# Second feed-forward of a two-layer flow step: products ordered around two row statistics

## The chip, the cores and the metric

The kernel runs on one core of a Trainium2 chip. The metric is the device time of one execution in microseconds (us). Five engines work side by side, each from its own queue in order: TensorE for matmuls (PE, with its weight loads as PEld), VectorE (DVE), ScalarE (ACT), GpSimd (POOL), and SyncE (SP), which issues most transfers. PE accumulates into PSUM, and DVE and ACT read the results from there. Everything is float32. A precise product is made of three matmuls: each operand is split into a rounded part ("hi") and a remainder ("lo"), and hi x hi, hi x lo and lo x hi are added up.

## The reference

One step of a hybrid backbone with two layers over 640 tokens (512 latent, 128 prompt) and a width of 1024. The first layer mixes by attention, the second by a gated linear recurrence; each is followed by a SwiGLU feed-forward with 2816 hidden columns. The change lies in the second layer's feed-forward and in the final norm behind it:

```python
def _rms_norm(x, g):
    xf = x.astype(jnp.float32)
    y = xf * lax.rsqrt(jnp.mean(xf * xf, axis=-1, keepdims=True) + RMS_EPS)
    return (y * g.astype(jnp.float32)).astype(x.dtype)

def _modulate(x, g, shift, scale):
    return _rms_norm(x, g) * (1 + scale[:, None, :]) + shift[:, None, :]

def _swiglu(x, w_gu, w_down):
    gate, up = jnp.split(x @ w_gu, 2, axis=-1)
    return (jax.nn.silu(gate) * up) @ w_down
...
        f_l = _swiglu(_modulate(lat, norm_g[i, 1], sh2_l, sc2_l), ffn_w_gu[i], ffn_w_down[i])
        ctx = ctx + g2_c[:, None, :] * f_c
        lat = lat + g2_l[:, None, :] * f_l
    y_prompt = _rms_norm(ctx, final_g)
    y_sample = _rms_norm(lat, final_g)
```

## The kernel before

Activations lie transposed: the 1024 features as 8 tiles of 128 partitions, the tokens along the free axis. The stages run one after another: attention, first feed-forward, recurrence, second feed-forward. Weights arrive as 512 KB blocks in the buffers `raw` (three of them), and ACT makes the rounded part, DVE the remainder.

**Who sets the order.** The program is written as one sequence. A planner then gives each engine its queue: among the instructions that its own estimate of time holds ready, it takes the one that was written first. The queues are fixed before the run, and semaphores are set between engines where data demands it. `tc.issue_after(ins)` adds an order without data: what is written inside the block stands behind `ins` on the same engine's queue. It adds no wait on another engine.

**The row statistic** (`stat`, line 376). The squares of the 8 feature tiles are made by ACT (`square`, L371) and added by DVE into `ssq` (L373); the last tile's square stays apart as `lastq`. For every 128 tokens, two matmuls with a column of ones sum over the partitions into the PSUM tile `at` (L382 for `ssq`, L385 for `lastq`). DVE makes the variance `var` (L387), POOL takes it to the power -0.5 (L389, `rs`), DVE spreads it on a diagonal `dg` (L391), and matmuls with ones (L394) put the factor on all partitions in a PSUM tile.

**The opening of the second feed-forward** (`project_halves`, then `ffn_halves`). The tokens are halved, 0 to 320 and 320 to 640, and each half has its own statistic. While the output projection of the second half ends, the first half is normalised already (`first_half`). Then the second statistic comes, ACT copies its factor to `rt` (L740), and `second_half` normalises the second half: 16 DVE products (`normed`, L691), 16 ACT shifts (L692), and the splits (`halve`, L1011 on ACT, L1012 on DVE).

The 22 hidden tiles are pairs of a gate tile and an up tile. The first two pairs (`PLAIN`) are multiplied in the usual way by `plain(us, c)` for token half `c`: four products of 24 matmuls per half (L835 to L837). From the third pair on a block scheme with seven instead of eight products is used (L779 to L781, `product`): `pair_a` needs the gate weights and the first token half alone, `pair_b` and `pair_c` need sums of weights, S1 to S4, and sums of activations, T1 to T4. `sums(k)` makes the T of feature tile k: L711 to L713 on DVE, one difference on POOL (L714), and four splits. `sum_weights` loads the up tile, makes the S with four operations (L762) and splits them into the buffers `whx`, `wlx`. For the third pair the S are made on DVE, behind the statistic's `dg` (argument `self.dg`); for all later ones on POOL, behind the operation kept in `self.pw`, which is the statistic's power.

In the written sequence stand: `plain` for the first half, `pair_a` of the third pair, `second_half`, `plain` for the second half, `sum_weights` of the third pair, `sums`; then for each pair `pair_b` and `pair_c`, and after every few pairs a part of the down projection (`project_part`).

**The end** (`project_last`). The last part of the down projection runs over 384 tokens, then over 256. Each group has its residual additions (L425 in `residual`), squares and a statistic. The final products (L466: x times factor times `final_g`, one per feature tile and token group) stand behind `self.added`, the last residual addition written. Each two feature tiles leave with one transfer (L468).

Of the kernel before, what the change touches and what calls it, by code (L numbers as in the profile page):

```python
# [12 lines left out]
ALU = mybir.AluOpType  # L13
AX = mybir.AxisListType

P = 128
D = 1024
# [13 lines left out]
EPS = 1e-6  # L31
# [8 lines left out]
KH = KT // 2  # L40
# [3 lines left out]
PLAIN = 2  # L44
# [77 lines left out]
def _pieces(t0, t1):  # L122
    return [(s, max(a, t0), min(b, t1)) for s, a, b in ((0, 0, NLAT), (1, NLAT, NTOK)) if max(a, t0) < min(b, t1)]


class _Step:
# [249 lines left out]
    def stat(self, t0, t1):  # L376
        nc = self.nc
        bl = [min(b, t1 - P) for b in range(t0, t1, P)]
        n = len(bl)
        ps = self.ps()  # L380
        for j, b in enumerate(bl):
            nc.tensor.matmul(ps[:, j:j + 1], self.ssq[:, b:b + P], self.ones[:, 0:1], start=True, stop=not self.lastq)  # L382
            if not self.lastq:
                continue
            nc.tensor.matmul(ps[:, j:j + 1], self.lastq[t0][:, b - t0:b - t0 + P], self.ones[:, 0:1], start=False, stop=True)  # L385
        v = self.t([P, 8], F32, "var", 2)[:, 0:n]
        nc.vector.tensor_scalar(v, ps[:, 0:n], 1.0 / D, EPS, ALU.mult, ALU.add)  # L387
        r = self.t([P, 8], F32, "rs", 2)[:, 0:n]
        self.pw = nc.gpsimd.tensor_tensor(r, v, self.mhalf.broadcast_to([P, n]), ALU.pow).ins  # L389
        dg = self.t([P, 4, P], F32, "dg", 1, self.sb)[:, 0:n]  # L390
        self.dg = nc.vector.tensor_tensor(dg, self.ident.unsqueeze(1).broadcast_to([P, n, P]), r.unsqueeze(2).broadcast_to([P, n, P]), ALU.mult).ins  # L391
        ps = self.ps("rr" if "rr" in self.ptags else "mx")
        for j, b in enumerate(bl):
            mm = nc.tensor.matmul(ps[:, b - t0:b - t0 + P], self.ones, dg[:, j], start=True, stop=True)  # L394
        self.r = ps, t0
        return mm.ins
# [25 lines left out]
    def residual(self, f, t0, t1, ps, G, sq):  # L422
        for s, a, b in _pieces(t0, t1):
            xs = self.x[:, f, a:b]
            self.added = self.nc.vector.scalar_tensor_tensor(xs, ps[:, a - t0:b - t0], G[:, s, f:f + 1], xs, ALU.mult, ALU.add).ins  # L425
        if sq:
            self.square(f, t0, t1)

# [21 lines left out]
    def project_last(self, w, hi, lo, gk):  # L450
        G = self.need(self.gcols, gk)
        us, fin = [], []
        for f in range(0, KT, 2):
            us += self.two(w[f:f + 2], f % 4)
        for c, (t0, t1) in enumerate(CHL):
            for f, u in enumerate(us):
                with self.tc.issue_after(mm) if c and f == KT - 1 else nullcontext():
                    ps = self.chunk(u, hi, lo, t0, t1)
                self.residual(f, t0, t1, ps, G, True)
            mm = self.stat(t0, t1)  # L460
            fin.append((t0, t1, self.r[0]))
        for t0, t1, r in fin:
            for k in range(KT):
                xs = self.x[:, k, t0:t1]
                with self.tc.issue_after(self.added):
                    self.nc.vector.scalar_tensor_tensor(xs, xs, self.col("fg", k), r[:, 0:t1 - t0], ALU.mult, ALU.mult)  # L466
                if k % 2:
                    self.nc.sync.dma_start(self.o["y"][k * P - P:k * P + P, t0:t1].rearrange("(k p) t -> p k t", p=P), self.x[:, k - 1:k + 1, t0:t1])  # L468
# [217 lines left out]
    def normed(self, k, t0, t1, key):  # L686
        nc = self.nc
        A, B = [self.need(self.AB, key + (j,)) for j in range(2)]
        for s, a, b in _pieces(t0, t1):
            v = self.x[:, k, a:b]  # L690
            nc.vector.scalar_tensor_tensor(v, v, A[:, s, k:k + 1], self.rt[:, a:b], ALU.mult, ALU.mult)  # L691
            nc.scalar.activation(v, v, AF.Identity, bias=B[:, s, k:k + 1])  # L692

    def halve(self, n, k, v):
# [12 lines left out]
    def sums(self, k, xd):  # L707
        nc = self.nc
        b11, b12, b21, b22 = [self.x[:, j, a:a + HT] for j in (k, k + KH) for a in (0, HT)]
        t2 = self.t([P, HT], F32, "c22", 2, self.sb)  # L710
        nc.vector.tensor_tensor(b11, b12, b11, ALU.subtract)  # L711
        nc.vector.tensor_tensor(t2, b22, b11, ALU.subtract)
        nc.vector.tensor_tensor(b12, b22, b12, ALU.subtract)  # L713
        nc.gpsimd.tensor_tensor(b21, b21, t2, ALU.subtract)  # L714
        for n, v in (("T1", b11), ("T2", t2), ("T3", b12), ("T4", b21)):
            self.halve(n, k, v)
        for j in (k, k + KH):
            nc.sync.dma_start(self.x[:, j], xd[j * P:j * P + P])
# [50 lines left out]
    def last_weights(self, q):  # L769
        hi, lo = [self.t([P, KH, P], F32R, n, 1, self.sb) for n in ("wuh", "wul")]  # L770
        self.split(hi, lo, q["u"][:, KH:])
        q["W"]["A22"] = hi, lo

    def product(self, ps, W, X, start):
        nc = self.nc
        hi, lo = W
        xh, xl = self.X[X + "h"], self.X[X + "l"]
        for k in range(KH):
            nc.tensor.matmul(ps, hi[:, k], xh[:, k], start=start and k == 0, stop=False, skip_group_check=not start)  # L779
            nc.tensor.matmul(ps, hi[:, k], xl[:, k], start=False, stop=False, skip_group_check=not start)  # L780
            nc.tensor.matmul(ps, lo[:, k], xh[:, k], start=False, stop=(k == KH - 1), skip_group_check=not start)  # L781

# [43 lines left out]
        self.hidden(q["j"], 1, q["c22"], self.total(q["c"], q["u2"], "g"))  # L826

    def plain(self, us, c):
        nc = self.nc
        for j, pair in enumerate(us):  # L830
            for u, (hi, lo) in enumerate(pair):
                ps = self.pg()[:, 0:HT]
                for k in range(KT):
                    xh, xl = [self.X[f"B{1 + k // KH}{1 + c}{p}"][:, k % KH] for p in "hl"]
                    nc.tensor.matmul(ps, hi[:, k], xh, start=(k == 0), stop=False)  # L835
                    nc.tensor.matmul(ps, hi[:, k], xl, start=False, stop=False)
                    nc.tensor.matmul(ps, lo[:, k], xh, start=False, stop=(k == KT - 1))  # L837
                if u:
                    self.hidden(j, c, ps, g)
                else:  # L840
                    g = self.t([P, HT], F32, "g", 3, self.sb)
                    nc.scalar.activation(g, ps, AF.Silu)

    def ffn_halves(self, l, key, xd):
        us = [[self.unit(self.i["gu"][l, c * NF + f]) for c in range(2)] for f in range(PLAIN)]
        self.plain(us, 0)
        self.wx, self.share = 0, False
        qs = [None] * PLAIN + [self.gate_weights(l, PLAIN)]
        self.pair_a(qs[PLAIN])
        for k in range(KH):  # L850
            self.second_half(k, key)
        self.plain(us, 1)
        self.sum_weights(qs[PLAIN], self.dg)
        for k in range(KH):
            self.sums(k, xd)
        f0 = 0
        for ci, n in enumerate(CHN):
            for j in range(n):
                f = f0 + j
                if f < PLAIN:  # L860
                    continue
                if f == len(qs):
                    qs.append(self.gate_weights(l, f))
                    self.pair_a(qs[f])
                if j:
                    if f > PLAIN:
                        self.sum_weights(qs[f])
                    if qs[f - 1]:
                        self.pair_c(qs[f - 1])
                    self.last_weights(qs[f])  # L870
                self.pair_b(qs[f], j)
            self.pair_c(qs[f])
            w = self.i["dn"][l, :, :, f0:f0 + n]
            f0 += n
            if f0 == NF:
                self.share = True
                self.project_last(w, self.hhi, self.hlo, (l, 5))
            else:
                qs.append(self.gate_weights(l, f0))
                self.pair_a(qs[f0])  # L880
                self.sum_weights(qs[f0])
                self.last_weights(qs[f0])
                self.project_part(w, self.hhi, self.hlo, (l, 5))
# [280 lines left out]
```

## Time and profile before

| | us |
|---|---|
| median of 3 runs | 1559.88 |
| lowest and highest | 1555.52, 1560.43 |
| profiled execution | 1555.75 |
| its span, first to last instruction | 1554.0 |
| PE busy | 1486.2 (96%) |
| DVE busy | 1076.6 (69%) |
| ACT busy | 716.7 (46%) |
| POOL busy | 208.9 (13%) |

The mean granted TensorE clock over the span is 0.984. In a timeline each row has the start in us from the span's start, the duration in us, the engine, the line, the operation, the tile written and those read, the shapes, and how many like instructions were merged; in brackets stands how long the engine was idle before it, and who released it. A table of stretches gives for each stretch its length, the busy time and number of instructions of each engine asked for (in the order PE, PEld, DVE, ACT, POOL where all are), the granted clock, the busy share of the DMA engines and GB/s. The row of a group of transfers ends with the median time from issue to landing. Consecutive matmuls overlap, so their durations exceed the distance of their starts.

### The profile page before, as it was taken

What the parts mean: (1) busy time and instruction counts of PE and PEld (TensorE: products, weight loads), DVE (VectorE), ACT (ScalarE), POOL (GpSimd) and SP (SyncE); (2) the same over time, 40 slices, a digit from 0 to 9 for tenths busy, and PEclk for the clock granted to TensorE, in tenths of its full rate; (3) what the DMA queues carried; (4) which work ended last, traced back from release to release, by engine and by line L of the source; (5) the groups of instructions that cost most, each with busy time, mean ns of one, the idle gap of its engine ahead of it and who ended that gap; (6) DMA issues with size and microseconds to landing.
All of it is one profiled execution on the core that took longest, in us unless ns stands there. A gap on an engine that the chain in (4) does not pass through costs nothing.

```text
span 1554.0 us, 26047 instructions
## 1 busy us (share of the span) xinstructions
PE 1486.2 (96%) x10303; PEld 1439.7 (93%) x10303; DVE 1076.6 (69%) x2043; ACT 716.7 (46%) x1326; POOL 208.9 (13%) x231
## 2 busy tenths in 40 slices
PE   6999999989999999999999999969999999999996
PEld 4899999879999999999999888869899999999995
DVE  5678788959999987434446489875876665555645
ACT  4576666654332123212334499754544342425241
POOL 2111123100111110000000000000132323232300
PEclk8999999999999999999999999989999999999998
DMA  9545655535666664222223222124242231313111
GB/s 374 161 114 165 178 167 165 155 120 181 193 190 188 208 198 117 74 82 80 64 84 105 70 62 68 55 102 148 69 143 81 70 109 55 109 55 109 55 55 68
DMA packets 69753, 188.25 MB, mean 121 GB/s; under 512 B 7792, under 2 KB 23296, under 8 KB 69504
## 3 DMA queue, kind: packets, MB, share of 16 engines
q1 hardware_dynamic: 57824, 144.49, 29.7%
q0 software_dynamic: 11520, 41.95, 8.8%
q8 instruction: 81, 1.33, 0.4%
q14 instruction: 40, 0.33, 0.1%
q10 hardware_dynamic: 288, 0.16, 0.0%
HBM read 171.09 MB, written 8.92 MB: 116 GB/s over the span
## 4 chain that ended last, share of the span: by engine, by line
PE 79%; DVE 7%; ACT 7%; DMA 3%; issue 3%; POOL 1%; SPq 0%; POOLq 0%; DVEq 0%; ACTq 0%
PE mm L209 13%; PE mm L210 13%; PE mm L211 13%; PE mx L211 5%; PE mx L210 5%; PE mx L209 5%; PE mx L779 3%; PE mx L780 3%; PE mx L781 3%; PE op L629 2%; PE tp L553 1%; PE mc L779 1%; PE mc L781 1%; PE mc L780 1%; PE mm L225 1%
## 5 line engine op out<-in xcount | busy, mean ns | idle before, releaser
L209 PE MATMUL mm<-big,whi 128*128 128x320 f32 (+2 forms) x1290 | 401.2, 314 | 19.0 <-ACT big L1011 10.4
L210 PE MATMUL mm<-big,whi 128*128 128x320 f32 (+2 forms) x1290 | 403.7, 313 | 1.7 <-DVE big L1012 1.2
L211 PE MATMUL mm<-big,wlo 128*128 128x320 f32 (+2 forms) x1290 | 402.4, 313 | 1.0 <-DVE wlo L178 1.0
L209 PEld LDWEIGHTS mm<-big,whi 128*128 128x128 f32 x1290 | 244.2, 190 | 24.2 <-ACT big L1011 11.3
L210 PEld LDWEIGHTS mm<-big,whi 128*128 128x128 f32 x1290 | 245.2, 190 | 4.9 <-DVE big L1012 3.7
L211 PEld LDWEIGHTS mm<-big,wlo 128*128 128x128 f32 x1290 | 244.9, 190 | 2.5 <-DVE wlo L178 1.4
L239 DVE SCALAR_TENSOR_TENSOR mprod<-mraw,csb 128x1024 f32<-128x1024 f32 x160 | 195.8, 1224 | 14.4 <-DMA mraw<-in_wm 13.6
L425 DVE SCALAR_TENSOR_TENSOR x<-mm,G,x 128x128 f32<-128x128 f32 (+3 forms) x211 | 84.9, 435 | 88.2 <-PE mm L211 87.3
L177 ACT CAST whi<-raw 128x1024 fp32r<-128x1024 f32 (+1 forms) x89 | 92.3, 1037 | 111.8 <-PE mm L210 79.0
L178 DVE TENSOR_TENSOR wlo<-raw,whi 128x1024 fp32r<-128x1024 f32 (+1 forms) x89 | 109.1, 1226 | 28.3 <-ACT whi L177 25.8
L211 PE MATMUL mm<-big,wlx 128*128 128x320 f32 (+3 forms) x363 | 112.6, 311 | 0.0
L210 PE MATMUL mm<-big,whx 128*128 128x320 f32 (+3 forms) x363 | 112.6, 310 | 0.0
L209 PE MATMUL mm<-big,whx 128*128 128x320 f32 (+3 forms) x363 | 112.4, 310 | 0.0
L235 POOL DMA_DIRECT2D mraw<-in_wm x80 | 43.3, 542 | 385.1 <-DVE mprod L239 271.0
L389 POOL TENSOR_TENSOR rs<-var,mhalf 128x3 f32<-128x3 f32 (+3 forms) x10 | 9.2, 926 | 584.1 <-DVE var L387 584.1
L209 PE MATMUL mx<-big,whi 128*128 128x320 f32 (+3 forms) x278 | 86.6, 312 | 1.0 <-DVE big L638 1.0
L211 PE MATMUL mx<-big,wlo 128*128 128x320 f32 (+3 forms) x278 | 86.3, 310 | 0.0
L210 PE MATMUL mx<-big,whi 128*128 128x320 f32 (+3 forms) x278 | 86.2, 310 | 0.0
L177 ACT CAST whx<-raw 128x1024 fp32r<-128x1024 f32 (+1 forms) x39 | 40.0, 1028 | 89.3 <-PE mm L210 54.3
L211 PE MATMUL mx<-big,wlx 128*128 128x320 f32 (+3 forms) x245 | 76.1, 310 | 0.4 <-DVE wlx L178 0.4
L210 PE MATMUL mx<-big,whx 128*128 128x320 f32 (+3 forms) x245 | 75.8, 309 | 0.0
L209 PE MATMUL mx<-big,whx 128*128 128x320 f32 (+3 forms) x245 | 75.7, 309 | 0.0
(283 smaller groups left out, 3622.2 us busy)
## 6 DMA issues: line engine op xcount, KB each, us to landing
raw<-in_gu SPq DMA_DIRECT2D x88, 512.0 KB, 3.6
mraw<-in_wm POOLq DMA_DIRECT2D x80, 512.0 KB, 4.0
raw<-in_dn SPq DMA_DIRECT2D x24, 512.0 KB, 3.7
raw<-in_wqk SPq DMA_DIRECT2D x16, 512.0 KB, 5.1
raw<-in_wi SPq DMA_DIRECT2D x16, 512.0 KB, 3.5
raw<-in_dn SPq DMA_DIRECT2D x16, 448.0 KB, 3.3
sw<-in_wm SPq DMA_DIRECT2D x10, 512.0 KB, 10.6
raw<-in_wv SPq DMA_DIRECT2D x8, 512.0 KB, 3.8
```

Source lines behind the costliest of these rows:

```text
L177: nc.scalar.copy(hi, raw)
L178: nc.vector.tensor_tensor(lo, raw, hi.bitcast(F32), ALU.subtract)
L209: nc.tensor.matmul(ps, hi[:, k], xhi[:, k, s], start=(k == 0), stop=False)
L210: nc.tensor.matmul(ps, hi[:, k], xlo[:, k, s], start=False, stop=False)
L211: nc.tensor.matmul(ps, lo[:, k], xhi[:, k, s], start=False, stop=(k == nk - 1))
L235: nc.gpsimd.dma_start(w, self.i["wm"][l * 6 + j - 2, f])
L239: nc.vector.scalar_tensor_tensor(prod, w, 1.0, self.csb[:, s], ALU.mult, ALU.mult, accum_out=out[:, s, f:f + 1])
L425: self.added = self.nc.vector.scalar_tensor_tensor(xs, ps[:, a - t0:b - t0], G[:, s, f:f + 1], xs, ALU.mult, ALU.add).ins
L629: mm = nc.tensor.matmul(out, v, w, start=start, stop=stop)
L779: nc.tensor.matmul(ps, hi[:, k], xh[:, k], start=start and k == 0, stop=False, skip_group_check=not start)
L780: nc.tensor.matmul(ps, hi[:, k], xl[:, k], start=False, stop=False, skip_group_check=not start)
L781: nc.tensor.matmul(ps, lo[:, k], xh[:, k], start=False, stop=(k == KH - 1), skip_group_check=not start)
```

## The change

Three orders are altered; no arithmetic, buffer or transfer is added or removed.

1. The final products (L466) stand behind the variance of the last statistic written (`self.var`) instead of behind the last residual addition.
2. In `plain` for the first token half and in `pair_a` of the third pair, the first matmul of each product stands behind the last L385 matmul of the second half's statistic (`self.at`). Of the very first product only the second half of the contraction does so; its first 12 matmuls stay free.
3. The third pair's S stand on DVE behind the last product of the normalisation (`self.last`) and are written after `sums(0)`. `self.pw` now also takes POOL's difference in `sums`, so that the fourth pair's S stand on POOL behind the last of the four differences.

```diff
-            nc.tensor.matmul(ps[:, j:j + 1], self.lastq[t0][:, b - t0:b - t0 + P], self.ones[:, 0:1], start=False, stop=True)
+            self.at = nc.tensor.matmul(ps[:, j:j + 1], self.lastq[t0][:, b - t0:b - t0 + P], self.ones[:, 0:1], start=False, stop=True).ins
...
-        nc.vector.tensor_scalar(v, ps[:, 0:n], 1.0 / D, EPS, ALU.mult, ALU.add)
+        self.var = nc.vector.tensor_scalar(v, ps[:, 0:n], 1.0 / D, EPS, ALU.mult, ALU.add).ins
...
-            self.added = self.nc.vector.scalar_tensor_tensor(xs, ps[:, a - t0:b - t0], G[:, s, f:f + 1], xs, ALU.mult, ALU.add).ins
+            self.nc.vector.scalar_tensor_tensor(xs, ps[:, a - t0:b - t0], G[:, s, f:f + 1], xs, ALU.mult, ALU.add)
...
-                with self.tc.issue_after(self.added):
+                with self.tc.issue_after(self.var):
                     self.nc.vector.scalar_tensor_tensor(xs, xs, self.col("fg", k), r[:, 0:t1 - t0], ALU.mult, ALU.mult)
...
-            nc.vector.scalar_tensor_tensor(v, v, A[:, s, k:k + 1], self.rt[:, a:b], ALU.mult, ALU.mult)
+            self.last = nc.vector.scalar_tensor_tensor(v, v, A[:, s, k:k + 1], self.rt[:, a:b], ALU.mult, ALU.mult).ins
...
-        nc.gpsimd.tensor_tensor(b21, b21, t2, ALU.subtract)
+        self.pw = nc.gpsimd.tensor_tensor(b21, b21, t2, ALU.subtract).ins
...
+    def held(self, here):
+        return self.tc.issue_after(self.at) if here and self.hold else nullcontext()
+
...
         for k in range(KH):
-            nc.tensor.matmul(ps, hi[:, k], xh[:, k], start=start and k == 0, stop=False, skip_group_check=not start)
+            with self.held(k == 0):
+                nc.tensor.matmul(ps, hi[:, k], xh[:, k], start=start and k == 0, stop=False, skip_group_check=not start)
...
-        nc = self.nc
+        nc, first = self.nc, True
...
-                    nc.tensor.matmul(ps, hi[:, k], xh, start=(k == 0), stop=False)
+                    with self.held(k == (KH if first else 0)):
+                        nc.tensor.matmul(ps, hi[:, k], xh, start=(k == 0), stop=False)
...
+                first = False
...
+        self.hold = True
         self.plain(us, 0)
         self.wx, self.share = 0, False
         qs = [None] * PLAIN + [self.gate_weights(l, PLAIN)]
         self.pair_a(qs[PLAIN])
+        self.hold = False
         for k in range(KH):
             self.second_half(k, key)
         self.plain(us, 1)
-        self.sum_weights(qs[PLAIN], self.dg)
         for k in range(KH):
             self.sums(k, xd)
+            if k == 0:
+                self.sum_weights(qs[PLAIN], self.last)
```

## The prediction

> **What bounds the kernel now.** I read the page first, then the table of stretches around the second feed-forward's opening and around the end, then the timelines of TensorE (PE), VectorE (DVE), ScalarE (ACT) and GpSimd (POOL) in both places.
>
> ```profile
> span 1554.0 us, 26047 instructions
> PE 1486.2 (96%) x10303; PEld 1439.7 (93%) x10303; DVE 1076.6 (69%) x2043; ACT 716.7 (46%) x1326; POOL 208.9 (13%) x231
> ```
>
> PE is busy nearly throughout, so an edit gains only where PE stands or runs slowly. The change touches two such places. The first, in order of time on PE and DVE (start, duration, engine, line):
>
> ```profile
> 1090.04 0.30 PE L835 MATMUL mm<-big,whi 128*128 128x320 f32 x1
> 1098.54 0.28 PE L382 MATMUL at<-ones,ssq 128*128 128x1 f32 x2
> 1099.57 0.36 PE L385 MATMUL at<-ones,sq 128*128 128x1 f32 x2
> 1103.69 0.83 PE L394 MATMUL mx<-dg,ones 128*128 128x128 f32 x6
> 1113.61 0.63 PE L836 MATMUL mm<-big,whi 128*128 128x320 f32 x1 [3.66 <-DVE big L1012]
> ...
> 1093.37 1.08 DVE L373 TENSOR_TENSOR ssq<-ssq,sq 128x320 f32<-128x320 f32 x2
> 1101.63 0.68 DVE L762 TENSOR_TENSOR sum<-raw 128x512 f32<-128x512 f32 x1
> 1104.64 1.22 DVE L1012 TENSOR_TENSOR wlx<-sum,whx 128x1024 fp32r<-128x1024 f32 x1 [0.39 <-ACT whx L1011]
> 1105.78 6.96 DVE L691 SCALAR_TENSOR_TENSOR x<-x,A,r 128x192 f32<-128x192 f32 x16
> 1104.56 0.43 ACT L740 COPY r<-mx 128x320 f32<-128x320 f32 x1
> ```
>
> The squares are summed at 1093.37 + 1.08 = 1094.45, but the statistic's matmuls start at 1098.54: they stand in PE's queue behind products that were ready earlier. The normalisation (L691) starts at 1105.78, and PE runs dry waiting for it. What the dry spell costs is in the stretches (length, PE busy, count, granted clock, DMA):
>
> ```profile
> 1090.00:1098.50 8.50, 8.50 (x60) 1.00 0.24 83
> 1099.90:1103.70 3.80, 3.80 (x28) 1.00 0.00 0
> 1109.95:1113.60 3.65, 0.00 (x0) 0.86 0.00 0
> 1113.60:1118.00 4.40, 4.39 (x16) 0.50 0.00 0
> 1118.00:1119.40 1.40, 1.40 (x7) 0.50 0.00 0
> ```
>
> PE stands for 3.65 us and then runs at clock 0.50 for 5.8 us, in which it does 23 matmuls. At 3.80/28 = 0.136 to 8.50/60 = 0.142 us each these need 3.2 us, so 2.6 us are lost to the clock. The opening loses 3.65 + 2.6 = 6.25 us.
>
> The second place is the end:
>
> ```profile
> 1536.76 4.28 DVE L466 SCALAR_TENSOR_TENSOR x<-x,cols,mx 128x384 f32<-128x384 f32 x8
> 1540.95 0.42 DVE L373 TENSOR_TENSOR ssq<-ssq,sq 128x256 f32<-128x256 f32 x1
> 1541.29 0.60 DVE L425 SCALAR_TENSOR_TENSOR x<-mx,G,x 128x128 f32<-128x128 f32 x2
> 1544.82 0.16 DVE L387 TENSOR_SCALAR var<-at 128x2 f32<-128x2 f32 x1 [1.96 <-PE at L385]
> 1545.80 0.43 DVE L391 TENSOR_TENSOR dg<-ident,rs 128x256 f32<-128x256 f32 x1 [0.82 <-POOL rs L389]
> 1547.60 3.22 DVE L466 SCALAR_TENSOR_TENSOR x<-x,cols,mx 128x256 f32<-128x256 f32 x8 [1.38 <-PE mx L394]
> ...
> 1536.61 0.42 ACT L371 ACTIVATE sq<-x 128x256 f32<-128x256 f32 x1 [0.64 <-DVE ssq L373]
> ...
> 1542.92 0.58 PE L382 MATMUL at<-ones,ssq 128*128 128x1 f32 x2 [5.66 <-DVE ssq L373]
> 1544.22 0.56 PE L385 MATMUL at<-ones,sq 128*128 128x1 f32 x2
> ```
>
> PE's last product ends at 1542.92 - 5.66 = 1537.26. DVE, however, is inside eight final products of the first 384 tokens, 4.28 us, and takes up the last sums only at 1540.95.
>
> **The change part by part.**
>
> *Final products behind the second variance (L466).* The edge puts no semaphore in; it moves eight instructions on DVE's queue from before the last sums to after `var`. The sums then start when their square is there, 1536.61 + 0.42 = 1537.03, not at 1540.95: 3.9 us earlier. The last residuals move from 1541.29 to 1537.4, after PE's end at 1537.26, so that is allowed, and the statistic starts at about 1542.92 - 3.9 = 1539.0. Its four pairs took 1544.78 - 1542.92 = 1.86 us. They ran at the low clock; the first statistic's six pairs show the other price:
>
> ```profile
> 1527.39 0.28 PE L382 MATMUL at<-ones,ssq 128*128 128x1 f32 x2
> 1528.43 0.36 PE L385 MATMUL at<-ones,sq 128*128 128x1 f32 x2
> 1537.20:1542.90 5.70, 0.06 (x1) 0.00 (x0) 5.45 (x13) 0.72 (x2) 0.00 (x0) 0.68 0.72 260
> 1542.90:1546.40 3.50, 1.90 (x9) 1.84 (x9) 0.59 (x2) 0.00 (x0) 0.70 (x1) 0.50 0.07 26
> ```
>
> Six pairs in 1528.79 - 1527.39 = 1.40 us, so four need about 0.9. The wait is now 1.7 us instead of 5.66, and I take the full clock: `var` at 1539.95. What follows it on DVE is 0.16 + 4.28 + 0.43 + 3.22 = 8.1 us without a hole: the holes before `dg` (0.82) and before the second products (1.38) are covered by the 4.28. DVE ends at 1548.05 instead of 1547.60 + 3.22 = 1550.82: 2.8 us gained. At the low clock it is 1.8. So the end does not gain the 4.28: that work comes back after `var` and only fills 2.2 us of holes. The results leave in eight transfers, the larger four of them:
>
> ```profile
> out_y<-x SPq DMA_DIRECT2D x4, 384.0 KB, 2.5
> ```
>
> They now start after 1541 and follow one another at the pace of two products, 2 x 4.28/8 = 1.07 us. At 260 GB/s over a share of 0.72, hence some 360 GB/s when busy, one (0.393 MB) takes 1.09 us; they keep up, and what lies behind the last transfer stays as it is.
>
> *Products behind the statistic (L779, L835).* Again an order alone. Before the statistic there remain the first product's first twelve matmuls, 12 x 0.142 = 1.7 us from 1090.04. PE then waits from 1091.75 to 1094.45 for the squares: 2.7 us, a loss that was not there. Behind it are 108 matmuls (84 of the plain products, 24 of the third pair's), 15.3 us of cover at 0.142 for the chain through `var`, POOL's power, `dg`, L394, the copy and the normalisation.
>
> Does the wait halve the clock? The trace of before has two nearer gaps:
>
> ```profile
> 1018.00:1021.40 3.40, 0.68 (x5) 0.42 (x4) 2.15 (x3) 3.35 (x6) 0.00 (x0) 1.00 0.48 154
> 1021.40:1025.00 3.60, 3.60 (x25) 3.60 (x26) 3.30 (x4) 3.57 (x4) 0.00 (x0) 1.00 0.00 0
> 941.00:945.00 4.00, 0.99 (x4) 0.48 (x4) 4.00 (x4) 3.97 (x6) 0.00 (x0) 1.00 0.24 50
> 945.00:949.00 4.00, 4.00 (x14) 3.30 (x14) 3.66 (x7) 3.98 (x7) 0.00 (x0) 0.57 0.21 81
> ```
>
> About 2.7 us without work (3.40 - 0.68) left it at 1.00; about 3.0 (4.00 - 0.99) was followed by 0.57 over 4.0 us, which is 4.0 x 0.43/0.5 = 3.4 us at half and costs 1.7. Bounds: 0, and the 2.6 of the opening now. The wait of 2.7 is followed by a statistic of one-column matmuls that lasts 1.4 us, 4.1 us with hardly any work, so I take one such stretch, 1.7. The Trainium skill, "TensorE: Matmul & The Clock Gate", Part 1, says that the clock halves after an idle window of some 3.4 us that runs freely. If the statistic counts as work, that rule leaves the clock alone here; it is the first rival.
>
> The statistic then ends at about 1095.85 instead of 1099.93. L394 followed it by 3.76 us and some 26 matmuls; with half a clock for 3.4 us it comes at 1101.4 instead of 1103.69, the copy follows, and the normalisation starts at 1102.8, 3.0 us earlier. PE has done its 108 at about 1095.85 + 15.3 + 0.8 (L394) + 1.7 = 1113.7, and the 6.96 us of L691 with their ACT partners are nearly through by then, so the wait of 3.66 goes. Opening: 6.25 - 2.7 - 1.7 = 1.9 gained.
>
> *The third pair's sums behind the last normalisation.* Four DVE sums (0.68 each) and one `wlx` (1.22), 3.96 us, leave the gap in front of L691 and join a stretch in which DVE never rests:
>
> ```profile
> 1106.00:1128.90 22.90, 22.90 (x53) 0.85 0.20 57
> 1138.96 0.39 PE L209 MATMUL mm<-big,whi 128*128 128x320 f32 x1 [0.40 <-DVE g L798]
> ```
>
> In the gap they had cost only 1105.78 - (1104.56 + 0.43) = 0.8 us. Moved, they end DVE's list 3.96 - 3.0 = 1.0 us later, while PE comes 1.9 us earlier. PE's cover is the plain products of the second token half and the fourth pair's first products, 96 + 24 matmuls, 120 x 0.142 = 17 us from 1113.7 to 1131, when the list is through. I cost it at nothing; without the cover it costs up to 2.9. The raw buffers that these sums read are freed after 1102.8 + 6.96 = 1109.8 instead of from 1101.63 on, so the next two weight loads on SP's queue start some 8 us later; their users, POOL's sums and the first down projection, come after the cover as well.
>
> *The fourth pair's sums behind POOL's last difference.*
>
> ```profile
> 1126.98 3.91 POOL L714 TENSOR_TENSOR x<-x,c 128x320 f32<-128x320 f32 x2 [7.27 <-DVE c L712]
> 1133.89 1.47 POOL L762 TENSOR_TENSOR sum<-raw,raw 128x512 f32<-128x512 f32 x1 [3.00 <-DVE wlx L1012]
> 1135.33 1.54 POOL L762 TENSOR_TENSOR sum<-raw,sum 128x512 f32<-128x512 f32 x1
> ```
>
> L714 ends at 1130.89. Four sums by 1.3 to 1.5 us end at about 1136.5, a microsecond more if L714 moves with DVE; the last two ended at 1136.87 before, because they waited for `wlx`. Bounds -0.4 to +0.7, taken as nothing.
>
> **Sum.** 1.9 + 2.8 = 4.7 us. The profiled execution, 1555.75 us (span 1554.0), becomes 1551.0. It is near the lowest of the three runs, 1555.52; the median of 1559.88 lies 4.1 higher. I predict the median, 1559.88 - 4.7 = 1555.2. A measurement of this kernel tells about 0.3% from no change, here 4.7 us: the forecast stands on that line.
>
> **Rivals.**
> *The clock stays up before the statistic.* For it: the 2.7 us gap at 1.00. Against: the idle statistic behind it. The opening then gains 3.6, the sum is 6.4, and the time 1553.5. Chance 0.2.
> *DVE paces the third pair.* For it: 22.90 busy of 22.90, and PE's 0.40 wait on DVE. Against: 17 us of cover. PE meets a list 1.0 later, the opening loses 1.0, the sum is a gain of 1.8: 1558.1. Chance 0.22.
> *DVE's wait takes the clock down again.* If L394 stands so far back that L691 starts no earlier than 1105.8, the moved 3.96 us are all late; PE stands that long at the third pair's products, and the clock costs 2.6 as after the 3.66 wait. The opening loses 6.6, the end gains 1.8: 1564.7. It decides once L691 starts after 1104.5. Chance 0.16.
>
> **How the numbers follow.** The forecast has 0.42, with its own range 1553.5 to 1557. Half of it lies beyond 0.3%, half within. Faster: 0.21 + 0.2 and a little for a larger gain in runs nearer 1560, where the opening may cost more: 0.45. Same: 0.21 + most of the second rival's: 0.38. Slower 0.17. The range is 1550 to 1563: from the first rival less part of the runs' own spread (1555.52 to 1560.43) up to most of the last rival; about 0.1 is left out on each side.
>
> **What would show it.** Right: the statistic at about 1094.5, in front of it a PE wait of 2.5 us, L691 before 1104, no wait at L836 near 1110; at the end L466 after `var`, the last sums near 1537, DVE's work ending near 1548 on the old scale less what the opening gained. Wrong: clock at half for over 4 us after the statistic, PE waits on DVE in the third pair's products, or `dg` behind all eight products, which would put a new hole of 1.4 us before the last eight.

## The result, and the profile after

The changed kernel takes 1561.79 us (median of 16 runs, 1559.16 to 1563.59); the kernel before, timed beside it, 1556.51 us (16 runs, 1554.24 to 1560.67). The ratio is 1.0029, with a 95% interval from 1.0020 to 1.0038: some 4.5 us slower, where a gain of 4.7 us was forecast. The profiled execution took 1559.91 us, with the mean granted clock at 0.984 as before. The head of its page:

```profile
span 1558.1 us, 26050 instructions
PE 1487.4 (95%) x10303; PEld 1441.3 (92%) x10303; DVE 1077.2 (69%) x2043; ACT 718.1 (46%) x1326; POOL 207.5 (13%) x231
```

The engines do the same work; PE only stands more. To see where, I cut the span in two: from the first plain product of the second feed-forward to the end of PE's last product ("the stage"), and from there to the end of the span ("the end"). PE's last product ends where the idle time in front of the last statistic begins, for the kernel after at 1543.80 - 2.01 = 1541.79.

| us, from the profiled execution | stage | end |
|---|---|---|
| before | 1537.26 - 1090.04 = 447.22 | 16.74 |
| after | 1541.79 - 1091.06 = 450.73 | 16.31 |

So the stage lost 3.5 us and the end gained 0.4. (The first plain product itself starts 1.0 us later, but that lies ahead of everything that the change touches.)

The kernels differ by some lines, so that one statement has other numbers further down: the splits are L1012 before and L1021 after, the casts L1011 and L1020, the copy `snap` of a product out of PSUM on ACT L785 and L789; L718, the same in both, reloads a tile of x that the sums have overwritten, and L185 loads weights of the down projection.

The opening after the change, as a timeline of PE, DVE, POOL, SP's queue and ACT (start, duration, engine, line, operation, tile written and read; in brackets the idle time in front and who ended it):

```profile
1091.06 0.30 PE L840 MATMUL mm<-big,whi 128*128 128x320 f32 x1
1095.52 0.38 PE L382 MATMUL at<-ones,ssq 128*128 128x1 f32 x2 [2.55 <-DVE ssq L373]
1144.80 0.63 PE L783 MATMUL mx<-xt,wuh 128*128 128x320 f32 x1 [4.11 <-ACT snap L789]
...
1103.53 4.57 DVE L691 SCALAR_TENSOR_TENSOR x<-x,A,r 128x192 f32<-128x192 f32 x15 [4.45 <-ACT r L740]
1132.98 1.58 DVE L1021 TENSOR_TENSOR big<-g,big 128x320 fp32r<-128x320 f32 x1
1137.48 1.57 DVE L1021 TENSOR_TENSOR xt<-x,xt 128x320 fp32r<-128x320 f32 x1
1138.98 0.95 DVE L1021 TENSOR_TENSOR wlo<-raw,whi 128x768 fp32r<-128x768 f32 x1
...
1131.71 1.00 POOL L714 TENSOR_TENSOR x<-x,c 128x320 f32<-128x320 f32 x1 [2.03 <-DVE c L712]
1132.67 1.54 POOL L762 TENSOR_TENSOR sum<-raw 128x512 f32<-128x512 f32 x1
1137.29 1.42 POOL L762 TENSOR_TENSOR sum<-raw,sum 128x512 f32<-128x512 f32 x1
...
1139.08 0.32 SPq L718 DMA_DIRECT2D x<-xd  x1
1139.95 0.90 SPq L185 DMA_DIRECT2D raw<-in_dn  x2
...
1143.59 0.83 ACT L1020 CAST whi<-raw 128x768 fp32r<-128x768 f32 x1 [3.80 <-DMA raw<-in_dn]
1144.33 0.74 ACT L789 COPY snap<-mx 128x320 f32<-128x320 f32 x2
```

The reader is to see two things. The first lines of PE and DVE are as forecast: a wait of 2.55 us at the statistic, L691 some 3 us earlier against the first product, and no wait near 1110. But 41 us later PE stands for 4.11 us in the third pair, at its product with T4, for an ACT copy (`snap`). That wait was not in the profile before, and nothing in the prediction has it. The stretches behind both waits, and two of the end, which come below (length, PE busy and count, granted clock, DMA share, GB/s):

```profile
1097.20:1100.00 2.80, 2.80 (x12) 0.50 0.00 0
1144.80:1147.80 3.00, 3.00 (x11) 0.50 0.37 94
1540.34:1543.75 3.41, 1.45 (x13) 1.00 0.00 0
1543.80:1545.70 1.90, 1.87 (x8) 0.50 0.00 0
```

Both waits are followed by a stretch at half clock. Added up: 2.55 for the first wait, at least 1.4 for its 2.80 us at clock 0.50, 4.11 for the second, at least 1.5 for its 3.00 us at 0.50: 9.6 us or a little more, against the 6.25 that the opening lost before. That is a loss of at least 3.3, and the stage table says 3.5.

How the same place stood before, as the chain of waits of the kernel before has it (start, us, what):

```profile
1133.89 2.99 POOL sum L762 x2
...
1136.90 4.07 DMA raw<-in_dn
...
1141.80 0.42 ACT snap L785
...
1142.26 0.42 PE mx L779
```

The chain from a weight load of the down projection over a cast and a `snap` to PE existed before, and it arrived just in time. The load was issued at 1136.90, and the product started at 1142.26. After the change the load is issued 3.05 us later, at 1139.95 (2.0 us later if both are counted from the first product). Before, it waited for POOL's last sum; after, SP's queue waits for DVE's `wlo`, since this load takes another buffer there.

The wait of 4.11 us has two parts. Counted from the first product, PE is through with the same 306 matmuls 2.5 us earlier than before (1140.69 - 1091.06 = 49.63, against 1142.16 - 1090.04 = 52.12), and the product with T4 starts 1.5 us later (53.74 against 52.22). So the opening did gain time; PE spends that gain waiting, and the late chain and the half clock behind it, some 1.5 us each, make up most of the loss.

The end, as a timeline of PE and DVE:

```profile
1543.80 0.59 PE L382 MATMUL at<-ones,ssq 128*128 128x1 f32 x2 [2.01 <-DVE ssq L373]
...
1545.71 0.16 DVE L387 TENSOR_SCALAR var<-at 128x2 f32<-128x2 f32 x1 [1.96 <-PE at L385]
1545.79 4.28 DVE L466 SCALAR_TENSOR_TENSOR x<-x,cols,mx 128x384 f32<-128x384 f32 x8
1549.98 0.42 DVE L391 TENSOR_TENSOR dg<-ident,rs 128x256 f32<-128x256 f32 x1
1551.78 3.22 DVE L466 SCALAR_TENSOR_TENSOR x<-x,cols,mx 128x256 f32<-128x256 f32 x8 [1.38 <-PE mx L394]
```

The last statistic does start 2.0 us after PE's last product instead of 5.66, 3.65 earlier. But its eight matmuls ran at clock 0.50 as before (the last stretch above; the one in front of it shows the clock still at 1.00 up to 1543.75), and `dg` stands behind all eight final products: it starts 1549.98 - 1545.71 = 4.27 us after `var`, where it was 1545.80 - 1544.82 = 0.98. The hole of 1.38 us in front of the last eight is there as before. 3.65 - 4.27 + 0.98 leaves a gain of 0.4.

### The profile page after: what moved, and what is told of

It reads as the page before. It is cut to its first block, busy times and chain, and to the rows that moved or that the text cites. A ratio compares the mean times of both kernels' runs of the same rounds, so it can differ in the third digit from the quotient of the medians.

```text
span 1558.1 us, 26050 instructions
## 1 busy us (share of the span) xinstructions
PE 1487.4 (95%) x10303; PEld 1441.3 (92%) x10303; DVE 1077.2 (69%) x2043; ACT 718.1 (46%) x1326; POOL 207.5 (13%) x231
## 4 chain that ended last, share of the span: by engine, by line
PE 80%; DVE 9%; ACT 7%; DMA 3%; issue 2%; POOL 0%; SPq 0%; DVEq 0%; ACTq 0%; POOLq 0%
PE mm L210 13%; PE mm L209 13%; PE mm L211 13%; PE mx L211 5%; PE mx L210 5%; PE mx L209 5%; PE mx L783 3%; PE mx L784 3%; PE mx L785 3%; PE op L629 2%; PE tp L553 2%; PE mc L783 1%; DVE big L1021 1%; PE mc L784 1%; PE mc L785 1%
```

## The experiments

The theories, once the result was known: (A) the order of the sums costs the time; (B) the tie of the products costs it, by its wait and the clock; (C) the end gives less than it seemed to, or takes. And, as to how A works: (A1) DVE paces the pairs, as in the second rival; (A2) DVE's splits are slowed by POOL's sums of the fourth pair beside them, and the weight load behind them comes late; (A3) the ACT queue, where the `snap` stands behind a cast that waits for its load. All ratios below are against the kernel before, on the same chip.

### One part at a time

**The end alone.** The kernel before with the first item of the change:

```diff
-                with self.tc.issue_after(self.added):
+                with self.tc.issue_after(self.var):
```

> The kernel before with the final products behind the last variance, nothing else. Theory: the products of the first 384 tokens move behind var as a block and dg stands behind all eight of them, so the statistic comes 3.9 us earlier but dg does not; from PE's last product to the end of the span about 16.3 us instead of 16.7, a gain of 0.4 us, not told from no change. Rival: dg goes ahead of most of the eight, and the end gains 2 to 2.8 us.

Measured: 0.9993 (0.9983 to 1.0003), 1556.70 against 1558.08 us. What follows PE's last product takes 15.57 us, a gain of 1.2. DVE there, and the stretch of the statistic (PE's busy time and count, clock, DMA):

```profile
1544.04 4.28 DVE L466 SCALAR_TENSOR_TENSOR x<-x,cols,mx 128x384 f32<-128x384 f32 x8
1548.24 0.42 DVE L391 TENSOR_TENSOR dg<-ident,rs 128x256 f32<-128x256 f32 x1
1550.03 3.22 DVE L466 SCALAR_TENSOR_TENSOR x<-x,cols,mx 128x256 f32<-128x256 f32 x8 [1.38 <-PE mx L394]
```

```profile
1542.80:1544.00 1.20, 1.10 (x8) 0.87 0.00 0
```

Here the same statistic behind the same 2.0 us wait ran in 1.10 us, mostly at full clock; in the kernel after it took 1.87. So C holds in this form: the end gains 0.4 to 1.2 us by when the clock falls, not 2.8, since `dg` behind the eight products keeps the hole.

**The products' tie alone**, third and fourth pair's sums and end as before:

```diff
+    def held(self, here):
+        return self.tc.issue_after(self.at) if here and self.hold else nullcontext()
...
-                    nc.tensor.matmul(ps, hi[:, k], xh, start=(k == 0), stop=False)
+                    with self.held(k == (KH if first else 0)):
+                        nc.tensor.matmul(ps, hi[:, k], xh, start=(k == 0), stop=False)
```

> The kernel before with only the products of the opening tied behind the statistic; the sums of the third and fourth pair stay where they were. Theory (late loads): the new PE wait of 4.1 us near 1141 comes from the sums that were moved, not from the tie; it is gone or under 1.5 us here, and the kernel is 1 to 4 us faster than before. Rival (the tie itself costs): PE's wait for the statistic and the half clock behind it are 2.5 + 1.7 us, PE waits near 1141 all the same, and the kernel is 2 to 4 us slower than before.

Measured: 0.9996 (0.9988 to 1.0005); stage 446.62, 0.6 less than before. B falls. On DVE, with the sums in the gap where they were:

```profile
1101.31 1.23 DVE L1020 TENSOR_TENSOR wlx<-sum,whx 128x1024 fp32r<-128x1024 f32 x1 [0.39 <-ACT whx L1019]
1102.92 6.71 DVE L691 SCALAR_TENSOR_TENSOR x<-x,A,r 128x192 f32<-128x192 f32 x15 [0.39 <-ACT r L740]
```

The first product starts at 1090.47 here, so L691 starts 12.45 us behind it; in the changed kernel, with the sums gone from the gap, it is 1103.53 - 1091.06 = 12.47. Moving the sums out of the gap made L691 no earlier at all: DVE just stands 4.45 us there.

**The sums alone**, without the tie and with the end as before:

```diff
-        nc.gpsimd.tensor_tensor(b21, b21, t2, ALU.subtract)
+        self.pw = nc.gpsimd.tensor_tensor(b21, b21, t2, ALU.subtract).ins
...
-        self.sum_weights(qs[PLAIN], self.dg)
         for k in range(KH):
             self.sums(k, xd)
+            if k == 0:
+                self.sum_weights(qs[PLAIN], self.last)
```

> The kernel before with only the sums of the third and fourth pair moved. Theory (late loads): the down projection's third and fourth loads are issued 1 to 3 us later than at 1136.9, PE waits for ACT's snap behind the cast of such a load near 1142, and the kernel is 2 to 5 us slower than before. Rival (the tie itself costs): within 1.5 us of before.

Measured: 1.0030 (1.0020 to 1.0040), 1562.61 against 1558.08 us; stage 452.84. A holds: this part alone costs what the whole change costs. PE's waits here are on DVE, the longest two:

```profile
1114.60 0.52 PE L836 MATMUL mm<-big,whi 128*128 128x320 f32 x1 [1.96 <-DVE big L1013]
...
1143.45 0.38 PE L209 MATMUL mm<-big,whi 128*128 128x320 f32 x1 [2.07 <-DVE g L798]
```

Without the tie the normalisation is not earlier, the moved sums make DVE's list late, and DVE paces (A1). In the changed kernel, where DVE has 3 us more, these waits are absent; the loss has the same size by another way. The three single ratios add up to +0.30 - 0.04 - 0.07 = +0.19%, each to about 0.1, against the +0.29 measured; within these intervals the parts may or may not add up.

**Tie and third pair's sums, fourth pair's as before.**

```diff
-        self.pw = nc.gpsimd.tensor_tensor(b21, b21, t2, ALU.subtract).ins
+        nc.gpsimd.tensor_tensor(b21, b21, t2, ALU.subtract)
```

(this against the changed kernel, with its first item undone as well)

> The kernel after without the tie of the fourth pair's sums on POOL and with the end as before: the opening's products behind the statistic and the third pair's sums behind the last normalisation. If POOL's sums of the fourth pair, now all behind the last difference, are what makes the loads late, the wait near 1141 falls from 4.1 to under 2 us and the kernel is at or below before. If the DVE work moved into the full stretch is what makes them late (the difference on POOL and the last T4 come later), the wait stays at 3 to 4 us and the kernel is 3 to 5 us slower than before, like the changed one.

Measured: 1.0037 (1.0022 to 1.0051), from 6 runs of this kernel; stage 453.67 (its profiled execution, 1566.72 us, is the slowest of the six). PE waits 1.94 us for a DVE split and 2.57 us for a `snap`. Leaving the fourth pair's sums without their order made it no better. On POOL:

```profile
1127.31 6.29 POOL L762 TENSOR_TENSOR sum<-raw 128x512 f32<-128x512 f32 x1 [7.38 <-DVE wlx L1021]
...
1135.79 1.12 POOL L714 TENSOR_TENSOR x<-x,c 128x320 f32<-128x320 f32 x1
...
1139.89 1.11 POOL L714 TENSOR_TENSOR x<-x,c 128x320 f32<-128x320 f32 x1
```

The sums now get in between POOL's differences (L714); the last difference starts 45.3 us after the first product (1139.89 - 1094.58) instead of 40.7 (1131.71 - 1091.06), and the splits of T4, which read it, come after that. The first sum takes 6.29 us here instead of 1.54; DVE works beside it without a pause, with splits of 0.47 us, so here POOL is the one that is held (as far as the durations on POOL, which are rough, show it). So once the third pair's sums have been moved, the fourth pair's cost time in either order.

### The chain to the late snap

In the changed kernel DVE runs four splits (L1021, a subtraction with two inputs in SBUF) beside POOL's four sums; they take 1.58 us three times and 1.57 (the first and the last are shown above). The kernel before has the same instruction beside POOL's two sums (1133.89 to 1136.87), and without one:

```profile
1133.73 0.48 DVE L1012 TENSOR_TENSOR big<-c,big 128x320 fp32r<-128x320 f32 x1
1134.13 1.59 DVE L1012 TENSOR_TENSOR xt<-x,xt 128x320 fp32r<-128x320 f32 x1
1135.64 1.58 DVE L1012 TENSOR_TENSOR big<-g,big 128x320 fp32r<-128x320 f32 x1
```

0.48 us becomes 1.58 us. The Trainium skill, "SBUF — State Buffer", section "Who interferes with whom", says that a VectorE instruction with two SBUF inputs contends with a GpSimd instruction that reads SBUF, the port pair they share being an exclusive lock, and not with one that only writes it. The trace agrees as to the first half; the next run but one is on the second. The last T4 split ends at 1137.48 + 1.57 = 1139.05; the reload of x (L718, on SP's queue) overwrites what it read and is issued at 1139.08. Behind that split on DVE's queue stands `wlo` of the down projection's second weight load (to 1138.98 + 0.95 = 1139.93), and behind that reload on SP's queue stands the third load (L185). The third load overwrites the buffer that `wlo` reads; SP's queue waits for it 0.5 us more, and the load goes out at 1139.95. Two experiments cut this chain at its two ends.

**The last link: the cast before the snap.** The changed kernel, with the casts of the third and fourth weight load placed behind the third pair's last `snap` on ACT:

```diff
-            for j, u in enumerate(self.two(w[f:f + 2], False)):
+            with self.tc.issue_after(u3) if f > 2 and u3 else nullcontext():
+                us = self.two(w[f:f + 2], False)
+            for j, u in enumerate(us):
...
-        self.nc.scalar.copy(s, ps)
+        self.snapped = self.nc.scalar.copy(s, ps).ins
```

> The changed kernel, with one more order: the casts of the third and fourth weight load of the first down projection stand on ACT behind the third pair's last snap. Theory (late loads through ACT's queue): PE's wait of 4.1 us before the products with T4 near 1141 was for a snap that stood behind a cast that stood behind a late load; it falls under 1 us, the half clock near 1144 goes, and the kernel is 3 to 6 us faster than the changed one, so within 2 us of before. Rival (DVE is simply late): the last splits of T4 or the sums of the fourth pair are what PE really lacks; the wait moves to another place, and the kernel stays 3 to 5 us slower than before.

Measured: 0.9992 (0.9982 to 1.0003), 0.37 points below the changed kernel's ratio; stage 446.81. The timeline of ACT and PE:

```profile
1141.04 0.76 ACT L791 COPY snap<-mx 128x320 f32<-128x320 f32 x2 [0.94 <-PE mx L787]
1144.07 0.83 ACT L1023 CAST whi<-raw 128x768 fp32r<-128x768 f32 x1 [2.27 <-DMA raw<-in_dn]
...
1141.52 0.41 PE L785 MATMUL mx<-xt,wuh 128*128 128x320 f32 x1 [0.52 <-ACT snap L791]
```

The load is as late as it was (its cast starts at 1144.07), but no `snap` stands behind it: PE's wait falls from 4.11 to 0.52, and the clock stays at 1.00 (1141.00 to 1145.00). The late cast as such costs nothing. A3 holds.

**The first link: POOL's sums beside DVE's splits.** The changed kernel, with the fourth pair's POOL sums cut to 8 of 128 columns, so that most of these sums are left out, and two memsets in front that fill the tiles:

```diff
+            for s in ss:
+                with self.tc.issue_after(after):
+                    nc.gpsimd.memset(s, 0.01)
...
+                    o, x, y = [t[:, :, 0:8] for t in (o, x, y)]
```

> The changed kernel, in which the fourth pair's four sums on POOL work on 8 of 128 columns, after two fills of their tiles with a constant (the output leaves these sums out; every other instruction stays). In the changed kernel each DVE split beside such a sum took 1.58 us instead of 0.48. Theory (POOL's sums slow DVE): the four splits near 1133 to 1139 come back to about 0.5 us, DVE's split of the second load, which frees its buffer, ends 3 to 4.5 us earlier, the third load follows it, PE's wait of 4.1 us falls under 1.5, and the kernel is 3 to 5 us faster than the changed one. Rival (DVE is late by its longer list alone): the splits stay long or the load stays late, and the kernel is within 2 us of the changed one.

Measured: 0.9997 (0.9985 to 1.0008), 0.32 points below the changed kernel's. POOL, DVE, SP's queue and PE:

```profile
1132.45 1.84 POOL L761 MEMSET sum<- 128x1024 f32 x2
...
1132.79 0.48 DVE L1029 TENSOR_TENSOR big<-g,big 128x320 fp32r<-128x320 f32 x1
1133.99 0.47 DVE L1029 TENSOR_TENSOR xt<-x,xt 128x320 fp32r<-128x320 f32 x1
1135.61 0.96 DVE L1029 TENSOR_TENSOR wlo<-raw,whi 128x768 fp32r<-128x768 f32 x1 [1.14 <-ACT whi L1028]
...
1134.49 0.32 SPq L718 DMA_DIRECT2D x<-xd  x1
1135.37 1.60 SPq L185 DMA_DIRECT2D raw<-in_dn  x2
...
1139.02 0.41 PE L789 MATMUL mx<-big,whx 128*128 128x320 f32 x1 [1.08 <-ACT snap L795]
1141.56 0.41 PE L789 MATMUL mx<-xt,wuh 128*128 128x320 f32 x1 [0.52 <-ACT snap L795]
```

The splits beside POOL's memsets take 0.48 and 0.47, as that page of the Trainium skill has it for a GpSimd instruction that only writes; the last T4 split ends at 1134.46, the reload follows at 1134.49 and the load at 1135.37, and the 4.11 falls to 1.08 + 0.52. So A2 holds as to the splits, and with A3 the loss is one chain.

How the load hangs on the splits has to be read with care, because here the loads take the buffers in another order. In the changed kernel SP's queue waits for `wlo` (until 1139.93) before the third load; POOL's sums are through at 1138.71 by then. Here it waits for POOL's last small sum (1135.09 + 0.26 = 1135.35) before the third load and for `wlo` (1135.61 + 0.96 = 1136.57) before the fourth. Counted from the first product, which is at 1089.34 here, the third load goes out 2.9 us earlier than in the changed kernel (46.03 against 48.89) and the load that follows `wlo` 1.6 us earlier (1136.59 - 1089.34 = 47.25). The run takes away most of POOL's work as well as the contention; how much of the 2.9 us the faster splits alone are worth was not separated.

### Looking for a faster order

**More free matmuls in front of the tie.** The kernel before with the tie, but with the first 30 matmuls of the plain products free instead of 12:

```diff
-                    nc.tensor.matmul(ps, hi[:, k], xh, start=(k == 0), stop=False)
+                    with self.held(not first and k == (0 if j else 2)):
+                        nc.tensor.matmul(ps, hi[:, k], xh, start=(k == 0), stop=False)
```

> The kernel before with the opening's products tied behind the statistic, but with 30 instead of 12 matmuls left free in front of it. The statistic still starts at about 4.4 us after the first product, when its squares are there; PE's wait of 2.5 us in front of it falls under 0.5 us and the half clock of 3.4 us behind it goes. If PE's wait and the clock are what the tie costs, this is 4.2 us faster than with 12 free ones, 0.2 to 0.35% faster than before. If the normalisation on DVE and ACT then limits, a new wait of 1 to 3 us appears near 1110 and the gain is 0 to 2 us.

Measured: 0.9992 (0.9982 to 1.0001). The wait in front of the statistic is 0.63 us, and no half clock follows; the stage is 445.79, 1.4 less than before. A wait of 1.75 on a DVE split comes up near 1115 in its place, which is also there in the combination below.

**The end with its hole filled.** Two final products behind `var`, the other six behind `dg`:

```diff
-                with self.tc.issue_after(self.added):
+                with self.tc.issue_after(self.var if t0 == 0 and k < 2 else self.dg):
```

> The kernel before with the final products split: two behind the last variance, the other six and the second group behind the diagonal dg. If dg behind all eight products is what kept the end from gaining, dg now follows var by about 1.2 us, no hole stands before the last eight products, and from PE's last product to the end of the span it is about 15 us instead of 16.3 to 16.7: 1.5 to 2.5 us faster than before. If the end is bound elsewhere (transfers, the clock), 0 to 0.5.

Measured: 0.9992 (0.9981 to 1.0002); end 14.40 us instead of 16.74. DVE:

```profile
1544.57 1.13 DVE L466 SCALAR_TENSOR_TENSOR x<-x,cols,mx 128x384 f32<-128x384 f32 x2
1545.62 0.42 DVE L391 TENSOR_TENSOR dg<-ident,rs 128x256 f32<-128x256 f32 x1
1545.95 6.37 DVE L466 SCALAR_TENSOR_TENSOR x<-x,cols,mx 128x384 f32<-128x384 f32 x14
```

The last fourteen products run without a hole: this is the DVE stream that the prediction had expected of the change, and its 2.3 us are near the 2.8 forecast.

**Both together.** The two edits above on the kernel before:

> Both together: 30 free matmuls in front of the statistic, and the end with two products behind the variance and the rest behind dg; the sums stay as before. If the two parts add up, the sum of the two gains, 2 to 6 us (0.1 to 0.4%) faster than before.

Measured: 0.9979 (0.9968 to 0.9989), 1554.74 against 1557.84 us, the lowest ratio of all, though not told from the 0.9982 of snap30_fill below. PE in its opening:

```profile
1098.07 0.38 PE L385 MATMUL at<-ones,sq 128*128 128x1 f32 x2 [0.63 <-ACT sq L371]
1118.25 0.46 PE L841 MATMUL mm<-big,whi 128*128 128x320 f32 x1 [1.75 <-DVE big L1020]
```

**The changed kernel, mended and with 30 free matmuls.** After with the casts behind the snap, and the 30:

> The changed kernel with both repairs of the opening: the casts of the two late loads behind the third pair's last snap, and 30 instead of 12 free matmuls in front of the statistic. The end is that of the change (products behind var). With the sums moved out of the gap the normalisation should start earlier than with the sums in it, so PE's wait near 1115 should stay under 1 us. If the two waits (2.5 us and 1.7 us of half clock before and behind the statistic) are worth what the trace says, it is 3 to 4 us faster than the changed kernel with the first repair alone, 0.25 to 0.35% faster than before. If DVE, with its moved sums, is then what PE waits for near 1140, it gains under 2 us.

Measured: 0.9991 (0.9981 to 1.0001). PE:

```profile
1138.78 0.41 PE L786 MATMUL mx<-big,whx 128*128 128x320 f32 x1 [1.53 <-DVE big L1024]
```

PE comes earlier and now waits for DVE's splits at POOL's sums; the second rival shows here. With the end's products split as above as well:

> The same with the end split as well: two final products behind the last variance, the rest behind dg. If the end's gain adds up, it is another 1 to 2 us faster, 0.3 to 0.45% faster than before, and the fastest kernel of the study.

Measured: 0.9982 (0.9972 to 0.9992), 1554.21 against 1557.53 us: no better than the version that leaves the sums where they were.

## Why the prediction was wrong

The direction was wrong: +4.5 us came for -4.7. Step by step.

- **The fourth pair's sums behind POOL's last difference.** "Bounds -0.4 to +0.7, taken as nothing": this is the step that failed. The sums end at 1137.29 + 1.42 = 1138.71, 1.8 us later than before (0.8 if both are counted from the first product), by itself near the bound. But I priced them as POOL's work alone. As one block of four they lie beside four of DVE's splits instead of two, each of which takes 1.1 us longer, and these splits hold `wlo` behind them on DVE's queue, and with it the weight load into the buffer that `wlo` reads, the cast and the snap: 4.11 us of PE, and at least 1.5 by the clock. The prediction quoted the two POOL rows of before and did not look up what DVE did in those 3 us: there stood 1.59 and 1.58 us for what takes 0.48. The chain of waits of before, which the prediction did not follow, led from exactly these POOL sums to PE with no time to spare. Cutting either end of the chain takes the loss back (after_snap, after_tiny).
- **The third pair's sums "at nothing".** Of the 0.8 us that they had cost in the gap, the move gave back nothing (12.47 against 12.45 us from the first product to L691), and without the tie it costs 0.3% (sums_only). With the tie, and the fourth pair's left alone, it costs 0.37% (hold_third). That "their users, POOL's sums and the first down projection, come after the cover as well" was said of the loads. It leaves out what these users do to others there: POOL's sums stand against DVE's splits, and the loads of the down projection against the `snap`.
- **The tie in the opening.** Right in its terms: wait 2.55 for 2.7, one stretch at half clock, L691 12.5 us after the first product for 12.8, no wait near 1110. A gain did come (PE is 2.5 us ahead at the product with T4 in the changed kernel), but the 1.9 did not last: with the tie alone the stage is 0.6 us shorter, the ratio 0.9996, since PE meets a wait of its own later (1.32 us on a DVE split, at 1133.68).
- **The end.** Of the 2.8 us, 0.4 came in the changed kernel's profile and 1.2 in that of the end alone. The last sums and the statistic moved up as said. The hole of 1.38 stayed, because `dg` was placed behind all eight products; the prediction named this among its signs of a wrong forecast, but its sum took the other order without a reason. The full clock that the sum took for the statistic came in one profile (1.10 us) and not in the other (1.87), behind waits of 2.00 and 2.01 us.
- **The clock rule.** That the clock would go down behind 2.7 us of waiting and a statistic of one-column matmuls was taken from the lengths of two gaps of before, and it came so: the granted clock is 1.00 from 1093.19 to 1096.60, 0.50 from there to 1100.01, and 1.00 again behind it. But the length of a gap alone doesn't decide it. In every trace here the stretches at 0.50 begin whole steps of 3.413 us apart; in the changed kernel they begin at 1096.60, 1144.39 and 1543.75, 14 and 117 steps from one to the next. The Trainium skill, "TensorE: Matmul & The Clock Gate", Part 1, has a window of some 3.4 us that runs freely, and the traces agree with that. It says that the clock halves after an idle window; here the step in front of 1543.75 held 1.45 us of PE's work, and the clock fell all the same, so a partly idle step was enough. The steps also explain the two outcomes behind the same wait of 2.0 us: the step ended 0.05 us before the statistic in the changed kernel (1543.75 against 1543.80) and 0.87 us into it with the end alone (1543.70 against 1542.83).
- **The rivals.** The third had the sign and even the size (a loss of 4.8, to 1564.7 from 1559.88), but by luck: its condition, L691 after 1104.5, did not come about. Its price was also mis-added: 3.96 + 2.6 = 6.6 for the opening leaves out the 1.9 gained there before, with which it would have read a loss of 2.9, 1562.8. The second rival, DVE pacing the pairs, shows in sums_only and snap30; in the changed kernel DVE's lateness reaches PE only by way of the load and the `snap`.
- **The range.** The 1561.79 measured lies within the 1550 to 1563 forecast. That is luck too: the kernel before, timed beside it, came out at 1556.51, 3.4 us under the median that the forecast starts from.

What stays open: how much of the 0.37% of hold_third is POOL's late differences and how much the slowed splits, and how much of the load's lateness in the changed kernel is due to the slowed splits alone. Neither was taken apart.

## What to carry to other kernels

Before work is moved on an engine that is not the bound, look at what the other engines do in the time it is moved to, and follow the chain of waits that runs through it: a chain with no time to spare shows no wait yet, and a step that "costs nothing" can be its first link. A transfer or a cast ahead of a critical copy in an in-order queue passes its lateness on to that copy; giving the copy its place ahead (after_snap) took the whole loss back. Where an order is written out to fill a hole, the far side of the hole has to be written out too, as end_fill does: work tied only to its start can be placed whole in front of what the hole waits for.

## What the hardware showed unexpectedly

- A DVE split of 128x320 with two SBUF inputs takes 0.48 us alone and 1.57 to 1.59 us beside POOL's sums of 128x512 (1.54 us each), about the time of the POOL instruction; beside POOL's memsets (two in 1.84 us) it stays at 0.47 to 0.48.
- The statistic's eight one-column matmuls behind an equal wait of 2.0 us took 1.10 us in one kernel (mean clock 0.87) and 1.87 us in another (0.50); behind a wait of 0.63 us the clock did not fall. A term that depends on this is known to about 0.8 us, not better.
- In these traces the clock falls only on steps of 3.413 us that run through the whole execution, wherever in a step the gap begins. In the kernel before, a step with 1.43 us of PE's work (1535.83 to 1539.24) was followed by 0.50 and one with 1.58 us (1017.00 to 1020.41) by 1.00; these are two cases, not a threshold.
